# Computing the eight gates of the first branch inside the attention loops of a two-block transformer kernel

## The chip, the cores and the metric

The kernel runs on one core of a Trainium2 chip. The metric is device time in microseconds (us) for one launch. The core has a matmul engine (TensorE: PE, with its weight loads listed as PEld), a vector engine (DVE), an activation engine (ACT), GpSimd (POOL) and a queue that issues transfers (SP). Each engine works through its own instructions in a fixed order and waits on semaphores for the others.

## The reference

The reference runs two different transformer blocks one after the other on 512 tokens of width 1024, in float32. The change is in the second one, which has two layers (l = 0 and 1). Cut to what matters, a layer is:

```python
h = rmsnorm(x, attn_norm[l])
(qA, kA, vA, fA, qB, kB, vB, qI, kI, wI, ..., gates) = split(h @ w_in[l])
yA = forgetting_attention(qA, kA, vA, fA, forget_bias[l])   # 8 heads, causal
yB = dsa_attention(qB, kB, vB, qI, kI, wI)                  # 8 heads, 128 selected keys a query
yC = head_groupnorm(retention(...)) * silu(gC)
yD = sliding_window_gqa(...)
branch = einsum('bsnc,ncd->bsnd', stack([yA, yB, yC, yD]), w_branch[l])
merged = sum(sigmoid(gates) * branch, axis=branches)        # a gate for each branch and feature
x = x + merged @ w_out[l]
```

The gates of the first branch, `sigmoid` of 512 x 1024 values, need only `h` and a slice of `w_in`. They do not need any attention.

## The kernel before, in words

Activations lie transposed: a tile has 128 features on the partitions and the 512 tokens along the row, so a width of 1024 is eight tiles. Every large product is split in three for precision: weights and activations are each cut into a high and a low part, and hi·hi, hi·lo and lo·hi are summed in one PSUM bank (`mm3`, lines 186 to 188 in the profile). One **gemm** of this text is one output tile: a transfer of 512 KB of weights (`raw`, 2 buffers), a cast to the high part on ACT (`hi`, L166), a subtraction on DVE (`lo`, L111), both with 3 buffers, and 24 matmuls of 128x128 by 128x512. Large products have four PSUM banks of the tag "mm".

In `mix2` a layer goes through these stages: rope projections for the indexer; the indexer's values `msc`; `natural(w_va)`; the **fox loop** (the forgetting attention, j = 0 to 3: two gemms, for keys and queries of two heads, and the preparation `fox_pair`); the **rope loop** (j = 0 to 3: one gemm and the preparation of two heads of the selected attention); then `branch(l, 0, ...)`, which makes the eight gates of branch 0 and its eight products. A gate is one gemm, a multiplication out of PSUM on DVE (`h<-psmm,g`, L111) and a Tanh on ACT. A product of a branch is half a gemm (12 matmuls) that needs all four head pairs of its attention, and its weights come two products to a transfer.

Attention is not written out at a place. `attend` is a generator that yields 14 times for a pair of heads: for each of four blocks of queries the scores and their row minimum (DVE L961), then Exp on ACT, reciprocal and scaling on DVE (L973, L975), then transposition on PE (L986) and a copy on ACT (L989), one block behind, and after the four blocks the 40 products with the values (L1000) and their split. `select` is another generator with 12 yields: three for the scores of query blocks 1 to 3, eight for two rounds each of finding and removing the eight largest values of every row (DVE L1123, L1124, 48 of each in a layer), one for turning the result into masks (L1129). `self.pump(4)` advances `select` by one step and the oldest attention pair by four. The pairs of the forgetting attention wait in a list ahead of those of the selected attention. `drain` runs a generator to its end.

The pumps, and with them the order in the program, come after each gemm of the fox loop, after each pair of the rope loop, and after each gate and each product. This order is a priority only: a scheduler that simulates the engines as it goes picks, for each engine, the first instruction in program order that can start then, as long as its buffers are free, and writes the order of every engine out. A later gate can so be placed ahead of an attention step that waits. Weights are taken from their buffers in about the order of the program.

In `branch`, `lead` gates (4 for branch 0) are issued first, then `drain(*gens)` finishes the pairs, and then each of the eight turns issues one more gate, as long as there are any, and one product.

Of the kernel before, what the change touches and what calls it, by code (L numbers as in the profile page):

```python
# [11 lines left out]
AF = mybir.ActivationFunctionType  # L12
# [5 lines left out]
P = 128  # L18
S = 512
D = 1024  # L20
KT = D // P
# [5 lines left out]
NL = 2  # L27
CHUNKS = 4
MAGIC = 12582912.0
LEAD = (4, 3, 3, 3)  # L30
NSLOT = 48
NSLOT2 = 12
NTMP = 10
# [38 lines left out]
class Builder:  # L72
# [1158 lines left out]
        for c in range(CHUNKS):  # L1231
            self.act(out[c][:, :ncol], banks[c][:, :ncol], AF.Copy, scale=self.rc[:, c:c + 1])

    def branch(self, l, n, y, x, first, gens=(), lead=3):


        nc = self.nc
        gs = []

        def gate(d):  # L1240
            bk = self.bank("mm")
            self.gemm_b(bk, self.weights(self.I["w_gates"][l, n, d], KT * P), x)
            g = self.merged[d] if first else self.tmp()
            self.mul(g, bk, self.rb)
            self.act(g, g, AF.Tanh, scale=0.5)
            gs.append(g)
            self.pump(self.rate)

        for d in range(lead):
            gate(d)  # L1250
        self.drain(*gens)
        wb = None
        for d in range(KT):
            if d + lead < KT:
                gate(d + lead)
            if d % 2 == 0:
                wb = self.weights(self.I["w_branch"][l, n, d // 2], 1024)
            bb = self.bank("mm")
            self.gemm_b(bb, wb, [y[j] for j in range(4)], off=(d % 2) * 512)
            g = gs[d]  # L1260
            nc.vector.scalar_tensor_tensor(g, g, 1.0, bb, ALU.add, ALU.mult)
            if not first:
                self.add(self.merged[d], self.merged[d], g)
            self.pump(self.rate)
# [33 lines left out]
    def mix2(self, l):  # L1298
        nc, ap, I = self.nc, self.ap, self.I
        self.rate = 1  # L1300
        wr = I["w_rope"][l]
        if self.x is None:
            x, fin = self.normed
        else:
            x, fin = self.rms_prep(self.x, f"g_attn{l}", S)
            for d in range(KT):
                nc.sync.dma_start(self.xd[d], self.x[d])
        b0 = self.project(wr[0], x)
        self.rb, self.rc = fin()
        self.cosR, self.sinR = self.g(), self.g()  # L1310
        self.mul(self.cosR, self.cload("cos"), self.rb)
        self.mul(self.sinR, self.cload("sin"), self.rb)
        self.merged = [self.g2() for d in range(KT)]
        proj = lambda n: self.rope(self.project(wr[n], x), self.tmp())

        hh, ll = self.stack_k(self.rope(b0, self.tmp()))
        si = self.stack_q(proj(2)) + self.stack_q(proj(3))
        msc = self.t(ap, [P, CHUNKS, 204], "msc")
        self.natural(I["w_misc"][l], x, [msc[:, c] for c in range(CHUNKS)], 204, 2)
        sel = self.select(si, hh[1], ll[1], msc)  # L1320
        self.bg2.append(sel)

        f = self.fox_bias(l, msc)
        self.rate = 4
        va = [self.g2() for _ in range(CHUNKS)]
        self.natural(I["w_va"][l], x, va, 512)
        self.fox_rows(f)
        ya, yb, yc, yd = {}, {}, {}, {}
        ga, gb, gd = [], [], []
        for j in range(4):  # L1330
            bk = self.project(I["w_fox"][l, 4 + j], x)
            self.pump(self.rate)
            bq = self.project(I["w_fox"][l, j], x)
            ga.append(self.fox_pair(ya, j, bq, bk, va))
            self.bg.append(ga[-1])
            self.pump(self.rate)

        for j in range(4):
            o = proj(4 + j)
            if j == 0:  # L1340
                self.drain(sel)
            gb.append(self.rope_pair(yb, j, self.stack_q(o), hh[0], ll[0],
                                     lambda c: self.maskc(c) if c == 0 else self.masks[c],
                                     lambda i: 3e38, lambda i, b: msc[:, b, 0:64],
                                     lambda c: list(range(c + 1))))
            self.bg.append(gb[-1])
            self.pump(self.rate)
        self.branch(l, 0, ya, x, True, ga, LEAD[0])
        self.rate = 2

        kd, kdl = self.stack_k(proj(1))
        nsk = self.t(ap, [P, 8], "nsk")
        nc.vector.tensor_scalar(nsk, self.vec(f"sink{l}"), -1.0, None, ALU.mult)
        for j in range(4):
            o = proj(8 + j)
            hg = j // 2
            gd.append(self.rope_pair(
                yd, j, self.stack_q(o), kd[hg], kdl[hg],
                lambda c: self.cs("maskw")[:, 128:] if c == 0 else self.cs("maskw"),
                lambda i, j=j: nsk[:, 2 * j + i:2 * j + i + 1],  # L1360
                lambda i, b, hg=hg: msc[:, b, 64 + hg * 64:128 + hg * 64],
                lambda c: [c] if c == 0 else [c - 1, c],
                lambda j: self.vec(f"sink{l}")[:, 2 * j:2 * j + 2]))
            self.bg.append(gd[-1])
            self.pump(self.rate)
        self.branch(l, 1, yb, x, False, gb, LEAD[1])

        vc = [self.g2() for _ in range(CHUNKS)]
        self.natural(I["w_vc"][l], x, vc, 512)
        sg = [self.g() for _ in range(CHUNKS)]  # L1370
        rn = self.g()
        nc.sync.dma_start(rn, I["ret_norm"][l].partition_broadcast(P))
        banks = self.gemm_a(I["w_gc"][l], x, 512, 4)
        for c in range(CHUNKS):
            g = sg[c]
            th = self.tmp()
            self.act(g, banks[c], AF.Copy, scale=self.rc[:, c:c + 1])
            self.act(th, g, AF.Tanh, scale=0.5)
            nc.vector.scalar_tensor_tensor(g, th, 1.0, g, ALU.add, ALU.mult)
            nc.vector.scalar_tensor_tensor(g, g, 0.5, rn, ALU.mult, ALU.mult)  # L1380
            self.pump(self.rate)
        q, k = [], []
        for lst, base in ((k, 12), (q, 16)):
            for j in range(4):
                lst.append(self.rope(self.project(wr[base + j], x), self.g()))
                self.pump(self.rate)
        gc = self.retain(yc, q, k, vc, sg)
        self.bg.append(gc)
        self.branch(l, 3, yd, x, False, gd, LEAD[3])
        self.branch(l, 2, yc, x, False, [gc], LEAD[2])  # L1390
        self.out_proj(I["w_out2"][l], self.xd)
# [202 lines left out]
```

## Time and profile before

| what | us |
|---|---|
| median of three runs | 3062.58 (3060.06 to 3064.8) |
| the profiled execution | 3062.15 |
| its span, first to last instruction | 3060.3 |
| PE busy in the span | 2985.7 |
| DVE busy | 1983.2 |
| ACT busy | 1353.1 |

An engine's busy time is the union of its instructions' times. Idle time of PE is what is left of a stretch. Granted clock is the share of its full clock that PE was given; a mean between one half and one means that a part of the stretch ran at each of the two levels. The fox loop of layer 0 begins near 1000 us of the span and its first branch ends near 1217; for layer 1 the same stages lie near 2045 to 2262.

### The profile page before, as it was taken

Reading aid. Unit: us, or ns where it says so; the run is one execution under the profiler, and the core shown is the slowest. Engines: PE = TensorE matmul, PEld = TensorE weight load, DVE = VectorE, ACT = ScalarE, POOL = GpSimd, SP = SyncE. Lnnn points to the kernel's source line nnn. Section 1 sums busy time; section 2 is a strip of 40 time slices with the busy share of each in tenths; the row PEclk is TensorE's granted clock in tenths of the full one; section 3 lists DMA queues with packets and bytes.
Section 4 is the critical chain, followed back from the end, with each engine's and each line's share of the span. In section 5 each row is a group of like instructions: output and inputs, shape, how many; then the busy total and the mean of one; then the engine's idle time right before and its main releaser. Section 6 shows DMA issues by size and latency. Waiting matters only on the chain.

```text
span 3060.3 us, 38946 instructions
## 1 busy us (share of the span) xinstructions
PE 2985.7 (98%) x14922; PEld 2486.8 (81%) x14922; DVE 1983.2 (65%) x3869; ACT 1353.1 (44%) x2276; POOL 116.6 (4%) x148
## 2 busy tenths in 40 slices
PE   8999899999999998999999999999899999999998
PEld 7888888888888877887888888888687788888887
DVE  7887664455447696566566566569856566665575
ACT  5523343422225565556234333356655453343343
POOL 0000000010010000000000010000000000000010
PEclk9999999999999999999999999999999999999999
DMA  5233452323333221222233323342122222323332
GB/s 164 85 95 97 109 162 80 104 90 99 102 92 124 88 76 42 69 78 89 69 107 113 97 90 103 89 140 76 56 66 66 87 80 81 125 88 100 99 95 81
DMA packets 98074, 287.09 MB, mean 94 GB/s; under 512 B 11984, under 2 KB 20432, under 8 KB 97888
## 3 DMA queue, kind: packets, MB, share of 16 engines
q1 hardware_dynamic: 97888, 284.61, 30.2%
q8 instruction: 117, 1.92, 0.3%
q14 instruction: 69, 0.57, 0.1%
HBM read 274.64 MB, written 9.93 MB: 93 GB/s over the span
## 4 chain that ended last, share of the span: by engine, by line
PE 89%; DVE 7%; ACT 2%; DMA 1%; issue 1%; SPq 0%; DVEq 0%; ACTq 0%
PE psmm L186 26%; PE psmm L188 26%; PE psmm L187 26%; PE pspv L1000 2%; PE pssc L986 1%; DVE g L111 1%; DVE lo L111 1%; DVE g L1124 1%; DVE m L1123 1%; DVE tmp L111 1%; DVE prob L961 1%; PE pssc L1089 1%; PE pssc L1090 0%; PE pspv L785 0%; PE pssc L753 0%
## 5 line engine op out<-in xcount | busy, mean ns | idle before, releaser
L186 PE MATMUL psmm<-g,hi 128*128 128x512 f32 (+1 forms) x3456 | 1343.3, 391 | 12.9 <-DVE g L111 3.8
L188 PE MATMUL psmm<-g,lo 128*128 128x512 f32 (+1 forms) x3456 | 1342.8, 389 | 3.5 <-DVE lo L111 3.5
L187 PE MATMUL psmm<-g,hi 128*128 128x512 f32 (+1 forms) x3456 | 1344.7, 389 | 0.0
L166 ACT CAST hi<-raw 128x1024 fp32r<-128x1024 f32 (+3 forms) x506 | 508.4, 1006 | 1177.1 <-PE psmm L187 827.4
L186 PEld LDWEIGHTS psmm<-g,hi 128*128 128x128 f32 x3456 | 649.8, 188 | 148.7 <-DVE g L111 4.0
L188 PEld LDWEIGHTS psmm<-g,lo 128*128 128x128 f32 x3456 | 650.6, 188 | 136.5 <-DVE lo L111 5.6
L187 PEld LDWEIGHTS psmm<-g,hi 128*128 128x128 f32 x3456 | 650.8, 188 | 130.5 <-issue 1.9
L111 DVE TENSOR_TENSOR lo<-raw,hi 128x1024 fp32r<-128x1024 f32 (+3 forms) x506 | 610.7, 1207 | 215.7 <-ACT hi L166 214.2
L111 DVE TENSOR_TENSOR tmp<-psmm,g 128x512 f32<-128x512 f32 x236 | 161.8, 689 | 294.2 <-PE psmm L188 274.4
L1440 DVE SCALAR_TENSOR_TENSOR g<-psmm,g 128x512 f32<-128x512 f32 x88 | 60.8, 690 | 149.1 <-PE psmm L188 149.0
L186 PE MATMUL psmm<-hi,g 128*128 128x512 f32 (+1 forms) x384 | 142.7, 380 | 13.5 <-ACT g L123 10.8
L111 POOL TENSOR_TENSOR tmp<-tmp,tmp 128x512 f32<-128x512 f32 x66 | 89.7, 1360 | 1535.2 <-DVE tmp L1414 979.4
L187 PE MATMUL psmm<-lo,g 128*128 128x512 f32 (+1 forms) x384 | 144.3, 379 | 0.0
L188 PE MATMUL psmm<-hi,g 128*128 128x512 f32 (+1 forms) x384 | 143.3, 378 | 0.0
L1414 DVE SCALAR_TENSOR_TENSOR tmp<-tmp,vec,tmp 128x511 f32<-128x511 f32 (+1 forms) x176 | 131.0, 746 | 2.0 <-ACT tmp L123 0.6
L111 DVE TENSOR_TENSOR g<-tmp,g 64x512 fp32r<-64x512 f32 (+2 forms) x166 | 113.4, 684 | 18.1 <-ACT g L166 11.0
L123 ACT ACTIVATE prob<-prob,nmx 128x128 f32<-128x128 f32 (+2 forms) x192 | 102.6, 535 | 45.5 <-DVE nmx L961 41.3
L989 ACT COPY probT<-pssc 128x128 f32<-128x128 f32 (+2 forms) x192 | 69.9, 399 | 73.2 <-PE pssc L986 72.4
L123 ACT ACTIVATE tmp<-tmp 128x512 f32<-128x512 f32 (+1 forms) x138 | 84.3, 613 | 24.5 <-DVE tmp L111 21.2
L986 PE MATMUL pssc<-idn,prob 128*128 128x128 f32 x432 | 71.2, 286 | 24.1 <-DVE prob L975 23.1
L186 PEld LDWEIGHTS psmm<-hi,g 128*128 128x128 f32 x384 | 73.7, 192 | 25.6 <-ACT g L123 10.8
L918 ACT COPY tmp<-psmm 32x512 f32<-32x512 f32 x160 | 92.5, 578 | 2.4
(271 smaller groups left out, 2694.8 us busy)
## 6 DMA issues: line engine op xcount, KB each, us to landing
raw<-w_up SPq DMA_DIRECT2D x110, 512.0 KB, 3.5
raw<-w_gates SPq DMA_DIRECT2D x64, 512.0 KB, 3.5
raw<-w_down SPq DMA_DIRECT2D x72, 384.0 KB, 3.1
raw<-w_rope SPq DMA_DIRECT2D x40, 512.0 KB, 3.6
raw<-w_branch SPq DMA_DIRECT2D x32, 512.0 KB, 3.5
raw<-w_out SPq DMA_DIRECT2D x24, 512.0 KB, 3.5
raw<-w_gate SPq DMA_DIRECT2D x22, 512.0 KB, 3.6
raw<-w_fox SPq DMA_DIRECT2D x16, 512.0 KB, 3.5
```

The costliest lines, as they stand in the source:

```text
L111: (eng or self.nc.vector).tensor_tensor(out, a, b, op)
L123: self.nc.scalar.activation(out, in_, func, **k)
L166: nc.scalar.copy(hi, src)
L186: mm(out, sh, mh, start=start, stop=False)
L187: mm(out, sh, ml, start=False, stop=False)
L188: mm(out, sl, mh, start=False, stop=stop)
L918: nc.scalar.copy(xs[k * 32:k * 32 + 32], bk[(k ^ 1) * 32:(k ^ 1) * 32 + 32])
L986: nc.tensor.transpose(tr[:, j * P:(j + 1) * P], pt[i][:, j * P:(j + 1) * P], self.ident)
L989: nc.scalar.copy(ptT, tr[:, :n * P])
L1000: nc.tensor.matmul(pv[i * 64:(i + 1) * 64, pc * P:(pc + 1) * P], value(i, b), tt[i][:, j * P:(j + 1) * P], start=j == 0, stop=j == len(bl) ...
L1414: nc.vector.scalar_tensor_tensor(o[:, sh:], u[:, :S - sh], w, o[:, sh:], ALU.mult, ALU.add)
L1440: self.nc.vector.scalar_tensor_tensor(self.x[d], ps, 0.5, self.x[d], ALU.mult, ALU.add)
```

## The change

A method `gate` takes over what the inner function of `branch` did. The fox loop issues one gate of branch 0 at the end of each turn, the rope loop too, so all eight exist when `branch(l, 0, ...)` starts; it gets them as `gs` and issues only the products. Each gate brings its pump along. The other three branches keep their lead of 3.

```diff
-LEAD = (4, 3, 3, 3)
+LEAD = {1: 3, 2: 3, 3: 3}
+    def gate(self, l, n, d, x, first):
+        bk = self.bank("mm")
+        self.gemm_b(bk, self.weights(self.I["w_gates"][l, n, d], KT * P), x)
+        g = self.merged[d] if first else self.tmp()
+        self.mul(g, bk, self.rb)
+        self.act(g, g, AF.Tanh, scale=0.5)
+        self.pump(self.rate)
+        return g
...
-    def branch(self, l, n, y, x, first, gens=(), lead=3):
+    def branch(self, l, n, y, x, first, gens=(), lead=0, gs=()):
-        for d in range(lead):
-            gate(d)
+        gs = list(gs)
+        while len(gs) < lead:
+            gs.append(self.gate(l, n, len(gs), x, first))
         self.drain(*gens)
         for d in range(KT):
-            if d + lead < KT:
-                gate(d + lead)
+            if len(gs) < KT:
+                gs.append(self.gate(l, n, len(gs), x, first))
...
             ga.append(self.fox_pair(ya, j, bq, bk, va))
             self.bg.append(ga[-1])
             self.pump(self.rate)
+            g0.append(self.gate(l, 0, len(g0), x, True))
...
             self.bg.append(gb[-1])
             self.pump(self.rate)
-        self.branch(l, 0, ya, x, True, ga, LEAD[0])
+            g0.append(self.gate(l, 0, len(g0), x, True))
+        self.branch(l, 0, ya, x, True, ga, gs=g0)
```

## Rows read from the trace of the kernel before

**Rows 1.** The page, part 1: busy time, share of the span, instructions.
```profile
PE 2985.7 (98%) x14922; PEld 2486.8 (81%) x14922; DVE 1983.2 (65%) x3869; ACT 1353.1 (44%) x2276; POOL 116.6 (4%) x148
```
**Rows 2.** Stretches: length, PE, PEld, DVE, ACT, POOL busy (instructions), clock, DMA share, GB/s.
```profile
700.00:750.00 50.00, 50.00 (x222) 41.42 (x221) 26.83 (x27) 14.10 (x17) 5.15 (x4) 1.00 0.32 95
...
1000.00:1040.00 40.00, 39.35 (x176) 31.72 (x175) 19.24 (x29) 12.81 (x20) 2.84 (x6) 1.00 0.29 96
...
1050.00:1100.00 50.00, 50.00 (x233) 41.54 (x232) 49.80 (x121) 33.34 (x60) 1.04 (x2) 1.00 0.27 86
1100.00:1150.00 50.00, 45.45 (x239) 36.77 (x236) 49.59 (x132) 32.47 (x63) 0.52 (x1) 0.97 0.23 74
...
1120.00:1150.00 30.00, 25.45 (x113) 19.92 (x112) 29.80 (x79) 17.98 (x34) 0.52 (x1) 0.94 0.22 71
1150.00:1195.00 45.00, 35.97 (x243) 29.39 (x243) 26.94 (x88) 26.43 (x73) 0.00 (x0) 0.85 0.04 12
...
2180.00:2200.00 20.00, 16.98 (x110) 12.99 (x108) 19.81 (x56) 11.11 (x26) 0.00 (x0) 1.00 0.21 68
2200.00:2240.00 40.00, 31.16 (x193) 25.82 (x193) 23.97 (x76) 22.73 (x62) 0.00 (x0) 0.83 0.00 1
```
**Rows 3.** Waits of PE, 1040 to 1240: total us, times, longest.
```profile
PE pssc L986 <- DVE prob L975: 8.7, 3, 4.3
...
PE psmm L186 <- DVE h L111: 1.8, 1, 1.8
```
**Rows 4.** Timeline of PE, 1100 to 1195: start, us, instruction, [idle before].
```profile
1105.58 2.40 PE L1000 MATMUL pspv<-probT,h 128*64 128x128 f32 x40
...
1148.95 1.04 PE L986 MATMUL pssc<-idn,prob 128*128 128x128 f32 x8
...
1151.98 2.40 PE L1000 MATMUL pspv<-probT,h 128*64 128x128 f32 x38
...
1167.57 1.97 PE L986 MATMUL pssc<-idn,prob 128*128 128x128 f32 x8 [4.25 <-DVE prob L975]
...
1171.56 3.19 PE L1000 MATMUL pspv<-probT,h 128*64 128x128 f32 x38
...
1187.42 3.77 PE L1000 MATMUL pspv<-probT,h 128*64 128x128 f32 x38
```
**Rows 5.** Groups of PE, 1150 to 1195, shapes apart: busy, mean ns, idle before.
```profile
L1000 PE MATMUL pspv<-probT,h 128*64 128x128 f32 x120 | 11.2, 332 | 0.3 <-ACT probT L989 0.3
L986 PE MATMUL pssc<-idn,prob 128*128 128x128 f32 x42 | 8.7, 336 | 8.7 <-DVE prob L975 8.7
L188 PE MATMUL psmm<-g,lo 128*128 128x512 f32 x12 | 4.7, 394 | 0.0
```
**Rows 6.** Timeline of SP's transfer issues, 1041 to 1211.
```profile
1041.38 22.74 SPq L174 DMA_DIRECT2D raw<-w_rope  x4
1068.02 24.34 SPq L174 DMA_DIRECT2D raw<-w_gates  x5
...
1128.64 0.33 SPq L174 DMA_DIRECT2D raw<-w_gates  x1
1135.94 6.57 SPq L174 DMA_DIRECT2D raw<-w_branch  x2
1152.16 59.09 SPq L174 DMA_DIRECT2D raw<-w_rope  x5
```
**Rows 7.** Groups of DVE, 990 to 1200, by line and tile.
```profile
L111 DVE TENSOR_TENSOR lo<-raw,hi 128x1024 fp32r<-128x1024 f32 x27 | 32.9, 1217 | 13.6 <-ACT hi L166 13.4
L1124 DVE MATCH_REPLACE8 g<-m,g 128x256 f32<-128x256 f32 (+2 forms) x48 | 25.8, 544 | 0.1
L1123 DVE MAX8 m<-g 128x8 f32<-128x256 f32 (+2 forms) x48 | 24.9, 550 | 0.1
...
L111 DVE TENSOR_TENSOR h<-psmm,g 128x512 f32<-128x512 f32 x8 | 5.4, 678 | 0.0
```
**Rows 8.** Timeline of DVE: the last mask of the selection in layer 0.
```profile
1150.57 0.42 DVE L1129 TENSOR_SCALAR g<-g 128x512 f32<-128x512 f32 x1
```
**Rows 9.** Groups of ACT, 1000 to 1250: the loads of activation tables.
```profile
L123 ACT ACT_TABLE_LOAD x1 | 1.3, 1283 | 0.0
```

More of the change, by code (lines that the diff above doesn't have):

```diff
@@ L1232, in natural @@
             self.act(out[c][:, :ncol], banks[c][:, :ncol], AF.Copy, scale=self.rc[:, c:c + 1])
-    def branch(self, l, n, y, x, first, gens=(), lead=3):
-        nc = self.nc
[L1238 to L1247, printed above, removed]
-        for d in range(lead):
-            gate(d)
+    def gate(self, l, n, d, x, first):
[7 more added lines that the diff above has]
+    def branch(self, l, n, y, x, first, gens=(), lead=0, gs=()):
+        nc = self.nc
+        gs = list(gs)
+        while len(gs) < lead:
+            gs.append(self.gate(l, n, len(gs), x, first))
         self.drain(*gens)
@@ L1328, in mix2 @@
         ya, yb, yc, yd = {}, {}, {}, {}
-        ga, gb, gd = [], [], []
+        ga, gb, gd, g0 = [], [], [], []
         for j in range(4):
```

## The prediction, made before the changed kernel was run

> **What bounds the kernel now.** The page's busy times come first: PE is busy for 2985.7 of 3060.3 us [rows 1], so the matmuls, which the change leaves alone, are nearly the whole time. Only two things can move: the 74.6 us in which PE idles, and stretches in which it works at the lower clock. So the second view is the table of stretches, and in it those between the fox loop and the end of branch 0. An undisturbed stretch holds 222 large matmuls in 50 us, 0.225 us each, so a gemm of 24 costs 5.4 us [rows 2]. In layer 0 PE is full up to 1120; from 1120 to 1150 it idles 4.55 us and from 1150 to 1195 another 9.0 us; in layer 1 the same place (2180 to 2240) shows 3.0 and 8.8 us [rows 2]. That is 25 of the kernel's 75 idle us in two short places, and both tails also show a granted clock of 0.85 and 0.83 [rows 2].
>
> What sets these two places differs, and the reader should see it in the DVE column. From 1050 to 1150 DVE is busy 99.4 of 100 us: 48 rounds of finding the largest values and 48 of removing them make 50.7 us there, beside the subtractions of all weights [rows 2, 7]. PE then waits for splits and for banks that DVE frees late (1.8 us the longest of that kind) [rows 3]. The last mask is done at 1150.6 [rows 8]. After that DVE is only 27 of 45 us busy [rows 2], and PE's long waits are three for the scaled probabilities, 8.7 us together [rows 3, 5]. The timeline of PE says why. The value products of the four fox pairs end at about 1108, 1154, 1175 and 1191 [rows 4]. Two whole pairs run behind the masks, one after the other, each a chain of scores, Exp, scaling, transposition and products that takes some 16 us (1171.6 to 1187.4), and nothing stands beside them: all gates have been consumed by then (the last of their transfers is issued at 1128.6, those of the branch's weights end at 1142.5), the DMA share is 0.04, and the weights of the branch fill the buffers while their products wait for these very pairs [rows 2, 4, 6].
>
> How much is lost in the tail? In 1150 to 1195 PE did 37 large matmuls (12 each of two forms and 13 of the third, of which the row shows one), 120 value products, 42 transpositions [rows 5], and 243 − 199 = 44 score matmuls [rows 2]. At undisturbed prices, 0.225, 2.40 / 38 = 0.063 and 1.04 / 8 = 0.13 us [rows 2, 4], with the scores at an estimated 0.13 (their mean width is near 300 columns, 300 / 512 of 0.225), this is 8.3 + 7.6 + 5.5 + 5.8 = 27.2 us of work in 45 us: **17.8 us lost, 9.0 of it idle and 8.8 by slow work**. The slow part is seen directly: eight transpositions take 1.97 us after the idle 4.25 us and 1.04 before, 38 products 3.77 against 2.40 [rows 4], so part of the tail runs at 1.2 instead of 2.4 GHz. The stretch from 1120 to 1150 lost 4.55 idle and about 0.06 × 30 = 1.8 by the clock, 6.4 us [rows 2]. Together 24 us in a layer, some 48 us in two.
>
> **The change part by part.** Nothing is computed that was not computed before: the same 8 gates with 8 transfers, 8 × 24 matmuls, 8 casts, 8 subtractions of 1.22 us, 8 multiplications of 0.68 us [rows 7] and 8 Tanh in a layer. The order changes, and with it what is beside what.
>
> Step 1, the pairs against the masks. Count the pumps. Before, the selection had its first step in `natural(w_va)`, eight in the fox loop, and the drain after the first rope gemm did the rest; 7 × 4 = 28 of the 56 fox steps stand before the last mask in the program, which fits two pairs left behind 1150 [rows 4, 8]. After, each turn of the fox loop pumps three times, so the twelve steps of the selection end at the eleventh pump, with 9 × 4 = 36 fox steps ahead. 20 steps are left instead of 28. If the tail's loss goes with the steps left, 17.8 × 8 / 28 = **5.1 us** go. Bounds: nothing, if the pairs wait for something else, and 17.8.
>
> Step 2, filler beside the rest. Before, one gate and the drain stood behind the last fox step, and the five gates after it were pulled forward. After, behind the last mask stand gate 3, the four rope gemms with gates 4 to 7: nine gemms, 49 us of PE work by 5.4 us each; behind the last fox step still gate 5, rope 2, gate 6, rope 3 and gate 7, 27 us. But the scheduler pulls forward whatever can start, as it did with the gates, so a part will be gone by the time of the tail. I take half of the remaining 12.7 us as covered, **6.3 us**; the bounds are 0 (all pulled ahead) and 12.7. On the clock the trace shows the fall only where PE had idled: 4.25 us before the slow transpositions [rows 4]. The Trainium skill, "TensorE: Matmul & The Clock Gate", section "What's actually happening", says that the throttled state is the default and activity releases it; the trace agrees. By that rule a filled wait gives back the slow work behind it as well, and the sum stands; if only idle time were given back, steps 1 and 2 would be worth about half, 5.7 us in place of 11.4.
>
> Step 3, what DVE pays. DVE's total does not change, and it was full from 1050 to 1150 [rows 2]. The gates 0 to 3 now claim 4 × (1.22 + 0.68) = 7.6 us of it ahead of the last masks, where the rope gemms' work moves behind. DVE had 20.8 idle us in 1000 to 1040 [rows 2], but the four "mm" banks hold only one gate beside the first three fox gemms there. So the stretch from 1120 to 1150 keeps its loss of 6.4 us; I charge one more stall of the measured kind, **1.8 us** [rows 3], between 0 and 7.6.
>
> Step 4, the rest at nothing. The 4 gate transfers that go ahead of fox transfers are 512 KB like those, and the DMA share was 0.2 to 0.3 there [rows 2], so PE's 5.4 us a gemm hides them; without that cover each would cost its wait for landing. No other transfer of SP is passed, and POOL's queue has no gate work. Tanh already runs among the Exps with a single table load in 1000 to 1250 [rows 9]; one more would be 1.3 us on an ACT that is 13 of 40 us busy in 1000 to 1040 [rows 2]. Branch 0 has no gate gemms of its own any more, but had consumed them earlier anyway. By the end of branch 0 both orders have pumped the same number of times, so what follows starts as before.
>
> The sum: 5.1 + 6.3 − 1.8 = 9.6 us a layer, 19 in two. 3062.15 (the execution's own time, 0.4 below the median of the runs) − 19 = **3043 us**. By the bounds: all of 2 × 24 saved gives 3014; nothing saved and 7.6 paid twice gives 3077.
>
> **The rivals.** *A. The tail is filled wholly*: the pairs run beside gates and rope gemms, and the masks are off the path. For it: nine gemms stand behind the last mask. Against it: the scheduler consumed eight gates early before. With both tails gone, 2 × 17.8: 3027, at best 3014.
>
> *B. No change.* DVE bounds this stage from 1040 to 1150 and does the same work; fillers are pulled ahead as before, and the tail keeps its shape. For it: PE's losses there are DVE's. Against: DVE idles 18 us in the tail [rows 2]. It gives 3062.
>
> *C. Slower, by DVE's queue.* Gates 0 to 3 stand in front of fox keys and queries and between rounds of the selection, at a time when PE had lost almost nothing (39.35 of 40 us busy [rows 2]), so they fill no gap; each puts 1.9 us into a DVE that is 99% busy, and a split waits for its cast with the rounds stuck behind it: 13.4 of DVE's idle us are such waits [rows 7]. The masks come 7.6 us later in a layer, the rope pairs that need them follow, the two pairs' tail stays: 3062 + 15 = 3077. It decides if the last mask lies later than 1158 while two value products still lie behind it. The Trainium skill, "TensorE: Matmul & The Clock Gate", section "Architectural detail: the array is 16× 32×32, not 1× 128×128", says that ACT and DVE take their queues strictly in order, the rule that speaks against this change. The waits just named agree with it.
>
> **How the numbers follow.** The forecast (3030 to 3056) has 0.43, A 0.18, B (within 6 us, the 0.2% that a measurement can just tell) 0.20, C 0.19. Faster is the first two, 0.61. The range leaves out the far ends of A and C: 3018 to 3072.
>
> **What would show it.** Right: the clock in both tails near 1.00, PE idle there under 5 us, weight transfers issued during the last two fox pairs, and the value products of pair 3 within about 16 us of those of pair 2 but with large matmuls between them. Step 1 is wrong if two value products still follow the last mask; step 2 if transfers pause there again; step 3 if PE's waits for `lo` and for DVE's multiplications grow by more than 4 us a layer. The prediction fails altogether if losses of the same size appear in branch 0, where the rope pairs now have only products beside them.

## The result: slower, and the profile of the changed kernel

The changed kernel takes **3081.06 us** (median of four, 3078.7 to 3082.54) where the kernel before takes 3061.77 beside it: 19.3 us more, a ratio of 1.0056 (95% interval 1.0044 to 1.0068). The forecast was 3043, the range ended at 3072, and even the upper bound of the sum, 3077, is passed. The profiled execution has a span of 3080.6 us against 3060.3.

The page, part 1, answers to [rows 1]:

```profile
PE 3001.8 (97%) x14922; PEld 2499.7 (81%) x14922; DVE 1985.5 (64%) x3869; ACT 1354.6 (44%) x2276; POOL 116.9 (4%) x148
```

With the same 14922 matmuls PE is busy 16.1 us longer and idles 78.8 in place of 74.6 us. Four fifths of the loss is thus slow work and not waiting. The stretches of the changed kernel (columns as in [rows 2]) say where:

```profile
1000.00:1040.00 40.00, 40.00 (x180) 32.49 (x179) 20.15 (x30) 13.93 (x19) 2.84 (x6) 1.00 0.29 94
1100.00:1150.00 50.00, 44.64 (x235) 36.62 (x233) 49.80 (x130) 31.62 (x60) 0.51 (x1) 0.95 0.24 74
1120.00:1150.00 30.00, 24.64 (x115) 19.96 (x113) 29.94 (x76) 16.04 (x31) 0.51 (x1) 0.92 0.28 88
1150.00:1195.00 45.00, 34.89 (x214) 28.46 (x215) 22.30 (x74) 27.62 (x72) 0.00 (x0) 0.73 0.00 1
1150.00:1200.00 50.00, 39.89 (x237) 32.52 (x237) 25.60 (x82) 31.45 (x81) 0.00 (x0) 0.74 0.00 0
1280.00:1340.00 60.00, 55.93 (x318) 45.42 (x318) 41.53 (x103) 33.27 (x76) 0.00 (x0) 0.97 0.20 62
2180.00:2200.00 20.00, 18.21 (x87) 14.82 (x86) 20.00 (x47) 10.92 (x21) 0.52 (x1) 1.00 0.30 87
2200.00:2240.00 40.00, 29.67 (x191) 23.57 (x192) 24.12 (x80) 27.80 (x70) 0.00 (x0) 0.84 0.03 10
```

and two stretches of the kernel before that were not shown yet:

```profile
1150.00:1200.00 50.00, 40.97 (x267) 33.52 (x267) 31.94 (x98) 30.46 (x82) 0.00 (x0) 0.86 0.05 12
1280.00:1340.00 60.00, 57.10 (x334) 46.67 (x333) 44.05 (x106) 33.09 (x78) 0.00 (x0) 1.00 0.22 71
```

The tail of layer 0 was to be filled; it is emptier. From 1150 to 1200 the DMA share is 0.00, the granted clock 0.74 against 0.86, and PE gets 237 matmuls done against 267. There is also a second place, 1280 to 1340, the tail of the selected attention's pairs, with 318 matmuls against 334.

The timeline of PE, 1100 to 1200, answers to [rows 4]:

```profile
1103.39 2.40 PE L1000 MATMUL pspv<-probT,h 128*64 128x128 f32 x40
...
1146.89 1.94 PE L986 MATMUL pssc<-idn,prob 128*128 128x128 f32 x8 [3.89 <-DVE prob L975]
...
1150.32 4.53 PE L1000 MATMUL pspv<-probT,h 128*64 128x128 f32 x38
...
1172.78 3.85 PE L1000 MATMUL pspv<-probT,h 128*64 128x128 f32 x38
...
1191.39 4.53 PE L1000 MATMUL pspv<-probT,h 128*64 128x128 f32 x38
```

The four value products end at 1106, 1155, 1177 and 1196 where they ended at 1108, 1154, 1175 and 1191; the last 38 take 4.53 us in place of 3.77. Groups of PE, 1150 to 1195 [rows 5], and its waits, 1000 to 1260 [rows 3]:

```profile
L1000 PE MATMUL pspv<-probT,h 128*64 128x128 f32 x114 | 13.7, 411 | 0.1
L986 PE MATMUL pssc<-idn,prob 128*128 128x128 f32 x40 | 8.0, 332 | 6.8 <-DVE prob L975 6.8
L188 PE MATMUL psmm<-g,lo 128*128 128x512 f32 x8 | 3.2, 394 | 0.0
```
```profile
PE pssc L986 <- DVE prob L975: 10.6, 5, 3.9
PE pssc L1077 <- ACT probT L989: 2.4, 1, 2.4
PE psmm L186 <- DVE h L111: 1.5, 1, 1.5
```

A value product costs 0.411 us on average in place of 0.332, and 8 large matmuls of a form stand in the tail where there were 12. The longest wait for a DVE multiplication out of a bank is 1.5 us (before 1.8). SP's issues [rows 6] and the last mask [rows 8]:

```profile
1116.22 0.33 SPq L174 DMA_DIRECT2D raw<-w_gates  x1
1123.93 12.30 SPq L174 DMA_DIRECT2D raw<-w_branch  x4
1143.15 73.14 SPq L174 DMA_DIRECT2D raw<-w_rope  x5
```
```profile
1149.91 0.42 DVE L1129 TENSOR_SCALAR g<-g 128x512 f32<-128x512 f32 x1
```

The last gate's weights are fetched at 1116.2, before 1128.6; the weights of the branch are all under way at 1136.2, before at 1142.5. The last mask lies at 1149.9, before 1150.6: it did not move.

One order did change, and ACT shows it (pairs are counted from 0). Each pair is prepared by casts (L1065 for a fox pair, L929 for a rope pair), and its result is cast after its last value product (`g<-pspv`, L166). Before, 1100 to 1200:

```profile
1108.03 0.59 ACT L166 CAST g<-pspv 128x512 fp32r<-128x512 f32 x1 [4.07 <-PE pspv L1000]
...
1118.67 0.61 ACT L1065 CAST g<-tmp 64x512 fp32r<-64x512 f32 x1
...
1132.42 0.62 ACT L1065 CAST g<-tmp 64x512 fp32r<-64x512 f32 x1
...
1154.41 0.59 ACT L166 CAST g<-pspv 128x512 fp32r<-128x512 f32 x1 [1.17 <-PE pspv L1000]
...
1155.36 1.26 ACT L929 CAST g<-tmp 64x512 fp32r<-64x512 f32 x2
...
1161.83 2.55 ACT L929 CAST g<-tmp 64x512 fp32r<-64x512 f32 x4
```

After:

```profile
1105.84 0.59 ACT L166 CAST g<-pspv 128x512 fp32r<-128x512 f32 x1 [2.86 <-PE pspv L1000]
...
1154.89 0.59 ACT L166 CAST g<-pspv 128x512 fp32r<-128x512 f32 x1 [3.63 <-PE pspv L1000]
...
1156.12 0.62 ACT L1065 CAST g<-tmp 64x512 fp32r<-64x512 f32 x1
...
1160.83 0.61 ACT L1065 CAST g<-tmp 64x512 fp32r<-64x512 f32 x1
...
1176.72 0.59 ACT L166 CAST g<-pspv 128x512 fp32r<-128x512 f32 x1 [3.01 <-PE pspv L1000]
...
1177.66 1.26 ACT L929 CAST g<-tmp 64x512 fp32r<-64x512 f32 x2
...
1196.02 0.59 ACT L166 CAST g<-pspv 128x512 fp32r<-128x512 f32 x1 [3.38 <-PE pspv L1000]
...
1197.01 1.91 ACT L929 CAST g<-tmp 64x512 fp32r<-64x512 f32 x3
```

The two casts at L1065 begin the two halves of one pair. Before, the last fox pair is prepared between 1118.7 and 1136 and all four rope pairs by 1164. After, the last fox pair is prepared only behind the result of pair 1 (1156 to 1167), rope pairs 0 and 1 behind that of pair 2 (1178), rope pairs 2 and 3 behind that of pair 3 (1197). In the code the results and the preparations take buffers of one tag, `g`, of which there are 48, handed out in program order; more pumps in the loops put a result ahead of the next preparation.

What the casts read was there long before. In the changed kernel the keys and queries of the last fox pair leave PSUM here (DVE):

```profile
1075.99 0.67 DVE L111 TENSOR_TENSOR tmp<-psmm,g 128x512 f32<-128x512 f32 x1
...
1082.61 0.69 DVE L111 TENSOR_TENSOR tmp<-psmm,g 128x512 f32<-128x512 f32 x1
```

The first cast starts at 1156.1, 73 us after the second of these, and from 1118.6, where the preparation of pair 2 ends, to the result of pair 1 at 1154.9 ACT is busy for only 18.4 of 36.3 us. So neither its inputs nor a busy ACT held this preparation back, and a scheduler that picks the first instruction that can start would have placed it earlier; what is left is the buffer that it writes.

### The profile page after: what moved, and what is told of

The parts are those of the page before. It is cut to its first block, busy times and chain, and to the rows that moved or that the text cites. A ratio compares the mean times of both kernels' runs of the same rounds, so it can differ in the third digit from the quotient of the medians.

```text
span 3080.6 us, 38943 instructions
## 1 busy us (share of the span) xinstructions
PE 3001.8 (97%) x14922; PEld 2499.7 (81%) x14922; DVE 1985.5 (64%) x3869; ACT 1354.6 (44%) x2276; POOL 116.9 (4%) x148
## 4 chain that ended last, share of the span: by engine, by line
PE 89%; DVE 6%; ACT 2%; DMA 1%; issue 1%; SPq 0%; DVEq 0%; ACTq 0%
PE psmm L186 26%; PE psmm L187 26%; PE psmm L188 26%; PE pspv L1000 2%; PE pssc L986 1%; DVE g L111 1%; DVE lo L111 1%; DVE g L1124 1%; DVE tmp L111 1%; DVE m L1123 1%; DVE prob L961 1%; PE pssc L1089 1%; PE pssc L1090 1%; PE pssc L695 0%; PE pspv L785 0%
## 5 line engine op out<-in xcount | busy, mean ns | idle before, releaser
L166 ACT CAST hi<-raw 128x1024 fp32r<-128x1024 f32 (+3 forms) x506 | 508.7, 1006 | 1180.7 <-PE psmm L187 823.3
L111 DVE TENSOR_TENSOR lo<-raw,hi 128x1024 fp32r<-128x1024 f32 (+3 forms) x506 | 610.8, 1207 | 221.9 <-ACT hi L166 220.5
L111 DVE TENSOR_TENSOR g<-tmp,g 64x512 fp32r<-64x512 f32 (+2 forms) x166 | 113.4, 684 | 20.8 <-ACT g L166 11.0
L986 PEld LDWEIGHTS pssc<-idn,prob 128*128 128x128 f32 x432 | 56.4, 149 | 46.3 <-DVE prob L975 13.2
```

The costliest lines, as they stand in the source:

```text
L111: (eng or self.nc.vector).tensor_tensor(out, a, b, op)
L166: nc.scalar.copy(hi, src)
L986: nc.tensor.transpose(tr[:, j * P:(j + 1) * P], pt[i][:, j * P:(j + 1) * P], self.ident)
```

## The experiments

Three theories. **O**: the early pumps put results ahead of preparations in that order, and the later pairs start late. **G**: the gates are spent early, so the tail has nothing beside it. **C**, the prediction's rival: DVE's full queue pays. All runs are timed beside the kernel before.

To place a loss, I compare the moments at which PE has done the same amount of work in two traces, each matmul counted at an undisturbed price (0.226 us for 512 columns, 0.062 a value product, 0.105 a transposition). Lag behind the kernel before in us, layer 0 counted from the start of its fox loop, layer 1 from where layer 0 had left it; "fox" is the end of branch 0 (near 1207 us), "rope start" behind the first waits of branch 1 (1354), "rope end" behind the two branches after it (1580):

```
                        layer 0: fox  rope start  rope end | layer 1: fox  rope start  rope end
the change                       6.1      9.7      11.3    |          1.9      7.0       9.5
gates without pumps              5.4      6.9      12.6    |          0.3      0.6       6.6
pumps without gates             -1.8      2.2       4.9    |          1.5      7.1       9.6
half pumps                      -4.2      0.8      -2.6    |         -2.1      3.2       0.0
change, half pumps               2.2      2.1      -0.4    |          2.3      4.0       1.4
change, filler                  -7.2      3.8       4.9    |         -5.1      2.2       2.3
half pumps, filler             -15.6     -6.7      -5.9    |        -13.8     -4.0      -3.0
the same, lead 5               -13.8    -11.7     -10.4    |        -12.9    -10.0      -8.9
before, half selection          -6.9     -6.9      -6.6    |         -9.4     -9.6      -8.0
change, half selection          -5.1     -0.1       0.0    |         -4.5     -2.0      -0.4
gates in the fox loop only       3.1      7.5       9.4    |          7.3     11.7      13.5
gates in the rope loop only      2.2      1.8       3.3    |         -0.3     -0.3       0.0
```

The last columns of both layers add up to the difference of the spans within 2.4 us in every row. Each row is one execution, and executions of one kernel lie up to 11 us apart (3057.13 to 3068.42 for the kernel before), so a difference of two or three microseconds counts for little unless both layers show it.

**Gates without pumps.** The gates go into the loops, their pumps stay in branch 0 (the new `False` turns the pump of a gate off; the pumps behind the products of branch 0 are doubled).

```diff
-            g0.append(self.gate(l, 0, len(g0), x, True))
+            g0.append(self.gate(l, 0, len(g0), x, True, False))
...
-            self.pump(self.rate)
+            self.pump(self.rate * (2 if first else 1))
```


> The gates stand in the loops as in the change, but no attention step is pumped with them; the eight pumps are made up in the branch. Theory O (buffer order): the pumps that came with the gates put the results of pair 1 ahead of the preparation of pair 3 in the order in which the 48 buffers are handed out; without them the preparation comes early again, as before the change: 3056 to 3068 us. Theory G (gates spent early): the gates are gone before the tail in which the last two pairs run alone: as slow as the change, 3075 to 3087 us.

Measured 3077.34 us, ratio 1.0053 (1.0040 to 1.0065): G's number. The last fox pair is prepared early again (1136.8), and yet the tail is as bare as the change's:

```profile
1150.00:1200.00 50.00, 42.05 (x248) 35.43 (x249) 28.30 (x95) 26.70 (x74) 0.00 (x0) 0.75 0.00 1
```

But only 5.7 us of it come by the end of branch 0 (5.4 and 0.3, so nearly all in layer 0), and 1.8 more by the rope pairs' start; 11.7 come behind that, where the change loses 4.1. The doubled pumps of branch 0, which only this kernel has, stand just before that place; whether they are the cause was not tested.

**Pumps without gates.** The gates stay in the branch and lose their pumps; each turn of the loops pumps once more, so that the number of pumps is the same.

```diff
-            self.pump(self.rate)
+            if not first:
+                self.pump(self.rate)
...
             self.bg.append(ga[-1])
             self.pump(self.rate)
+            self.pump(self.rate)
...
             self.bg.append(gb[-1])
             self.pump(self.rate)
+            self.pump(self.rate)
```


> The gates stay in the branch as before the change; the eight extra pumps of four steps are made in the loops. Theory O: as slow as the change, 3075 to 3087 us, with the preparation of fox pair 3 again behind the value products of pair 1 near 1155. Theory G: as fast as before, 3056 to 3068 us. If both count about half, e1 and e2 both lie near 3070.

Measured 3077.48, ratio 1.0049 (1.0037 to 1.0062): O's number. ACT shows the order of the changed kernel (the two halves of the last fox pair begin at 1150 and 1155, behind the result of pair 1). The tail keeps the clock and the transfers that it had before, and the second place is that of the changed kernel:

```profile
1150.00:1200.00 50.00, 39.35 (x226) 31.23 (x226) 32.06 (x90) 33.11 (x82) 0.00 (x0) 0.86 0.04 12
1280.00:1340.00 60.00, 55.19 (x316) 45.02 (x315) 43.41 (x104) 32.88 (x77) 0.00 (x0) 0.97 0.19 62
```

So both theories have their number. The table shows that they speak of different places: gates without pumps lose in branch 0 as the change does (5.4 and 0.3, change 6.1 and 1.9), pumps without gates lose nothing there (-1.8 and 1.5), and then, up to the rope pairs' start, 4.0 and 5.6 where the change loses 3.6 and 5.1.

**Half pumps, without and with the gates.** First the kernel before, then the changed one, with two attention steps a pump at every pump of both loops (the diffs show one of them).

```diff
-            self.pump(self.rate)
+            self.pump(2)
```


> The kernel before, with pumps of two steps instead of four in the two loops, so that all fox and rope preparations but one are handed their buffers ahead of the result of pair 1. Theory O: the rope pairs are ready earlier, faster than before by 3 to 12 us, 3050 to 3059. Theory G: the gates are consumed at about the same place, within 5 us of before, 3057 to 3067. If later attention steps cost more than early preparations give, slower, 3070 or more.

Measured 3057.86, ratio 0.9984 (0.9975 to 0.9993): less pumping in the loops is better even without the change. The time lies in O's range and, at its lower end, in G's too.

```diff
+            self.pump(2)
+            g0.append(self.gate(l, 0, len(g0), x, True, 2))
```


> The change, with all pumps of the two loops (the gates' too) of two steps instead of four, which gives about the number of steps of before at the same places. Theory O: 3055 to 3070 us, since fox pair 3 and the first two rope pairs are prepared ahead of the result of pair 1. Theory G: 3075 to 3087, since the gates are spent as early as in the change.

Measured 3062.49, ratio 1.0005 (0.9996 to 1.0014), in O's range: against the kernel before nothing is left of the 19 us that can be measured, although the gates stand where the change put them. Each pump also advances the selection by one step, and here there are as many pumps at the same places as in the change; so the earlier place of the selection in the program is not the cause. ACT casts rope pairs 0 and 1 (1139.6) ahead of the result of pair 1 (1157.5) and pairs 2 and 3 by 1165. The tail is still bare:

```profile
1150.00:1200.00 50.00, 43.07 (x269) 36.33 (x270) 30.19 (x103) 27.32 (x75) 0.00 (x0) 0.80 0.00 1
```

Its lag by the end of branch 0 is 2.2 and 2.3 us against the kernel before, but 6.4 and 4.4 against the half pumps without the gates, which is the fair comparison; of the times, 4.6 us remain (3062.49 against 3057.86). That is G's part. Behind branch 0 it has none of the change's loss.

**Where the gates stand.** All of the change in the fox loop (four gates there, four in the branch), or in the rope loop:

```diff
             self.bg.append(ga[-1])
             self.pump(self.rate)
+            g0.append(self.gate(l, 0, len(g0), x, True))
```


> Half of the change: four gates with their pumps in the fox loop, the other four one by one in the branch. Fox pair 3 is again prepared behind the result of pair 1. If that order and gates spent while PE is full make the loss: most of it is here, 3072 to 3082 us. If the place of the gates in the rope loop makes it: 3060 to 3068.


```diff
             self.bg.append(gb[-1])
             self.pump(self.rate)
+            g0.append(self.gate(l, 0, len(g0), x, True))
```


> The other half: four gates with their pumps in the rope loop, the other four in the branch. Fox pair 3 is prepared early as before, the rope pairs half as late as in the change. By buffer order and spent gates: 3060 to 3069 us; if the rope loop's gates make the loss: 3072 to 3082.

Fox loop alone 3077.61, ratio 1.0042 (1.0028 to 1.0056); rope loop alone 3064.97, ratio 1.0006 (0.9997 to 1.0015). It is the gates and pumps of the fox loop, and there the pumps stand ahead of the preparations of the next fox pairs: the fox loop's kernel casts its last fox pair from 1152 on, behind the result of pair 1 (1150.9), the rope loop's from 1120.

**Filler.** The change with three gates of branch 1 ahead of the products of branch 0:

```diff
+        g1 = [self.gate(l, 1, d, x, False) for d in range(3)]
         self.branch(l, 0, ya, x, True, ga, gs=g0)
...
-        self.branch(l, 1, yb, x, False, gb, LEAD[1])
+        self.branch(l, 1, yb, x, False, gb, LEAD[1], g1)
```


> The change, with three gates of branch 1 (which need no attention) issued ahead of the products of branch 0, 16 us of matmuls a layer that can run beside the last two fox pairs. Theory G (the tail is bare because the gates are spent): most of the tail's loss comes back, 3055 to 3070 us. Theory C (DVE's queue pushes the masks and pair 1 back): the added gates bring DVE work of their own, no gain, 3077 to 3090.

Measured 3068.38, ratio 1.0017 (1.0009 to 1.0026), in G's range, with 12.7 us of the change's loss won back and 6.3 left. The stretch 1100 to 1150 loses nothing now; the second place pays for it:

```profile
1100.00:1150.00 50.00, 50.00 (x261) 41.56 (x260) 49.81 (x125) 32.94 (x61) 0.52 (x1) 1.00 0.27 84
...
1280.00:1340.00 60.00, 54.09 (x295) 43.85 (x294) 42.18 (x102) 32.86 (x75) 0.00 (x0) 0.91 0.17 54
```

In the table PE is 7.2 us ahead at the end of branch 0 and 3.8 behind at the rope pairs' start: 11.0 of the gain are given back (7.3 in layer 1). The gates of branch 1 are the filler of its own tail; the last experiment tests this. Half pumps with the same filler and gates 4 to 7 of branch 0 ahead of its products:

```diff
+            self.pump(2)
+        g0 = [self.gate(l, 0, d, x, True) for d in range(4)]
+        self.drain(*ga)
+        g0 += [self.gate(l, 0, d, x, True) for d in range(4, KT)]
+        g1 = [self.gate(l, 1, d, x, False) for d in range(3)]
+        self.branch(l, 0, ya, x, True, ga, gs=g0)
```


> The kernel of the half pumps (gates in the branch), with the remaining gates of branch 0 and three gates of branch 1 ahead of its products. Theory G: the tail fills here too, 3040 to 3052 us. Theory C: 3055 to 3065.

Measured 3053.70, ratio 0.9969 (0.9956 to 0.9981), a miss for G's 3040 to 3052: 15.6 us ahead at the end of branch 0, 8.9 given back by the rope pairs' start.

**DVE's queue.** Both kernels with 8 of the 16 rounds of the selection; half of the selection is left out, and DVE's busy time falls by 44.1 us. Each round is now a step of its own, so the selection has as many steps as before.

```diff
-        for r in range(16):
+        for r in range(8):
```


> The kernel before with 8 of the 16 rounds of the selection left out, some 27 us of DVE work a layer. If DVE bounds the stage: 3030 to 3045 us. If the serial chain of the four fox pairs bounds it whatever DVE does: 3050 to 3060.

> The change with the same 8 rounds left out, to be read against e9. Theory C: with DVE relieved the gates' DVE work is free, the change costs under 8 us against e9. Theory G and the pumps' order: the tail of the last pairs and their late preparations stay, the change still costs 12 us or more against e9.

Before 3049.15, ratio 0.9956 (0.9943 to 0.9970), the change 3062.63, ratio 1.0001 (0.9992 to 1.0010). The kernel before lies between the two ranges named for it, just under the one of the serial chain. With half of the selection gone the change still costs 13.5 of its 19.3 us, so relieving DVE takes 5.8 of them away, and C is not the main cause. Both stretches from 1100 to 1150, the kernel before first:

```profile
1100.00:1150.00 50.00, 50.00 (x301) 41.40 (x300) 32.60 (x76) 37.09 (x77) 0.52 (x1) 1.00 0.24 74
```
```profile
1100.00:1150.00 50.00, 49.34 (x294) 40.86 (x293) 32.19 (x73) 37.84 (x75) 0.52 (x1) 1.00 0.24 74
```

DVE is 65% busy and PE full, or nearly, in both; they part company later, at the end of branch 0 (-6.9 against -5.1) and above all at the rope pairs' start (-6.9 against -0.1).

**Filler for both tails.** Half pumps with filler, and five gates instead of three ahead of the selected attention's drain:

```diff
-        self.branch(l, 1, yb, x, False, gb, LEAD[1], g1)
+        self.branch(l, 1, yb, x, False, gb, 5, g1)
```


> The half pumps with the three early gates of branch 1, and two more gates of branch 1 as a lead of that branch, ahead of the rope pairs' results. In the run without them most of the tail's gain was given back where branch 1 waits for the rope pairs. If filler is what is missing there too: 3042 to 3050 us. If the rope pairs' chain is pushed back by the gates: 3052 to 3060.

Measured **3040.96**, ratio 0.9929 (0.9916 to 0.9941): 21.6 us faster than the kernel before, 40.1 faster than the change, and 1 us better than the range for filler. Page and stretches:

```profile
PE 2980.5 (98%) x14922; PEld 2482.2 (82%) x14922; DVE 1983.3 (65%) x3869; ACT 1354.2 (45%) x2276; POOL 116.7 (4%) x148
```
```profile
1100.00:1150.00 50.00, 50.00 (x265) 41.62 (x265) 49.68 (x126) 25.71 (x49) 0.00 (x0) 1.00 0.26 85
1150.00:1200.00 50.00, 44.62 (x297) 36.06 (x296) 34.31 (x108) 28.14 (x76) 0.00 (x0) 0.93 0.11 32
1280.00:1340.00 60.00, 56.37 (x321) 45.57 (x321) 42.98 (x104) 31.75 (x76) 0.00 (x0) 1.00 0.21 67
```

The tail of layer 0 has transfers beside it (share 0.11), a clock of 0.93 and 297 matmuls; of the 13.8 us won in branch 0 only 2.1 are given back.

## Why the prediction was wrong

**What bounds the kernel** was read rightly: the loss sits in these two tails, part idle and part slow clock, and the last kernel won 21.6 us by filling them and the tail behind each (with half pumps, which alone win 4.4). What failed is what this change does to them: steps 1 and 2 were to save 11.4 us a layer, and by the end of branch 0 it is 6.1 and 1.9 us behind.

**Step 1** (eight more fox steps ahead of the masks, 5.1 us a layer) failed. The steps do stand earlier in the program, but two whole value products still follow the last mask, the sign that was named for it. Pair 1 ends at 1155, no earlier than before, and pairs 2 and 3 run behind it, one after the other. Pumps without gates are the clean test of this step: by the end of branch 0 they give 1.8 us in layer 0 and take 1.5 in layer 1, in place of 5.1 saved in each. The step counted program positions, and these are priorities; what the pumps did move was the handing out of buffers, and with that the preparation of the later pairs moved back.

**Step 2** (nine gemms of filler, 6.3 us a layer) failed, at its lower bound and beyond. The scheduler pulled every gate forward: The changed kernel has done near 1139 the work that the kernel before has done 8.3 us later, and then has nothing to put beside the pairs (a wait of 3.89 us before 1146.89). From 1150 to 1195 the transfers pause (0.00) and 8 large matmuls of a form stand there in place of 12. The bound of 0 meant "pulled ahead as before"; it was possible to have less than before, since the gates that the branch issued last were the latest independent gemms of this stage. By the end of branch 0 gates without pumps price it at 5.7 us in two layers; the times with half pumps price it at 4.6. On the clock the prediction's sentence holds: the slow work goes with the bare wait, and now it is 4.53 us for 38 products that cost 2.40 at the high level. By the rule of the Trainium skill, "TensorE: Matmul & The Clock Gate", section "What's actually happening", the throttled state is the default and activity releases it; the trace agrees, here in the direction of a loss (0.74 against 0.86).

**Step 3** and **rival C** (slower, 3077) came nearest in time (3077 for a measured 3081), but that is luck, since the loss has another reason. C's own deciding sign, a last mask later than 1158, is absent (1149.9); the waits for DVE's multiplications did not grow; and with 44 us of DVE's work left out 13.5 us of the cost remain.

**Step 4** held for transfers and tables, but not in its last sentence, that what follows starts as before because both orders have pumped as often by the end of branch 0. The rope pairs' preparations move from 1155 to 1164 to between 1178 and 1200, and the change loses 12.8 of its 20.8 us of lag behind branch 0 (3.6 + 1.6 and 5.1 + 2.5), a term that the sum put at nothing. Pumps without gates lose it too (4.0 + 2.7 and 5.6 + 2.5); the change with half pumps does not. The loss "of the same size" was foreseen as a condition of failure, for branch 0; the larger part lies one stage later.

The two causes do not simply add. Gates without pumps and pumps without gates each cost 15 us, 30 together, where the change costs 19.3. The early pumps' lag of 14.5 (4.9 and 9.6) and the gates' 5.7 by the end of branch 0 do make 20.2 beside the change's 20.8, but that leaves out the 13.5 us that gates without pumps lose later, so the agreement proves nothing. The times with half pumps give a cleaner chain: half pumps win 4.4, the gates with them cost 4.6, and whole pumps on top of that cost 18.6. The pumps are the main part.

**What stays open.** That the tag's 48 buffers are what holds the preparations is read from the code, from the order of casts, and from inputs that lie ready while ACT idles. It was not tried with buffers of their own for the results. Why gates without pumps lose 11.7 us behind the rope pairs' start is open. DVE's share of the cost, 5.8 us by the one pair of kernels, was not divided further.

## What to carry to other kernels

Ask of independent work that is moved forward not only what it fills, but what it filled where it stood: in front of a stage that waits on one serial chain, the filler is worth most when it is issued last, and a tail that is filled with the next tail's filler has to be paid there. Where steps of a chain are issued earlier in the program, follow its allocations from shared buffers, since a result that is late holds up every preparation allocated behind it. Read the order of the casts or copies that write those buffers, before and after; busy shares do not show it.

## What was not expected of the hardware

An engine that is full is not therefore the bound: from 1050 to 1150 DVE is 99.4 of 100 us busy [rows 2], yet taking 44.1 us off it in two layers won 13.0 us, while the last kernel, with DVE as full (49.68 of 50 us from 1100 to 1150), half pumps and more filler for PE, won 21.6. And a bare tail lengthens itself: from 1150 to 1200 the granted clock is 0.74, and the chain's own 38 products take 4.53 us in it where they take 2.40 at the full clock. Four fifths of the change's loss (16.1 of 20.3 us of span) is counted as busy time of PE.
